# Scores between transposes and values: one run of projection products per step of differential attention, and another order of the opening

## The chip, the cores and the metric

The kernel runs on one core of one Trainium2 chip. The metric is the device time of one execution in microseconds; lower is better. The engines of the core are called as in the profile: PE (TensorE's matmuls) and PEld (its weight loads), DVE (VectorE), ACT (ScalarE), POOL (GpSimd) and SP (SyncE, which here only issues DMAs).

## The reference

Two decoder layers over 512 tokens of width 1024, each followed by a gated ConvFFN. The change touches only layer 0, the even layer: latent attention (MLA, 8 heads) and differential attention (4 heads) run behind one input projection, and their outputs go through one output projection.

```python
def even_mixer(h, w_in, cq_g, w_uq, ckv_g, w_ukv, ...):
    c_q, c_kv, k_rope, dq, dk, dv = split_cols(h @ w_in, EVEN_SPLITS)
    q = heads_first(rms_norm(c_q, cq_g) @ w_uq, MLA_HEADS)
    kv = heads_first(rms_norm(c_kv, ckv_g) @ w_ukv, MLA_HEADS)
    o_mla = mla_attention(q_nope, q_rope, k_nope, rope(k_rope, pos), v_mla)
    ...
    o_diff = diff_attention(dq[:, :, 0], dq[:, :, 1], dk[:, :, 0], dk[:, :, 1], dv, lam, slopes)
    o_diff = rms_norm(o_diff, subln_g) * (1.0 - lam_init)
    return jnp.concatenate([heads_last(o_mla), heads_last(o_diff)], axis=-1) @ w_out

def diff_attention(q1, q2, k1, k2, v, lam, slopes):   # per block of 128 queries
    p = probs(a1, k1) - lam * probs(a2, k2)           # two causal softmaxes with ALiBi
    return p @ v
```

## The kernel before

Weights and activations of the large products are split into two float32r parts, high and low, and a product is three matmuls: high by high, high by low, low by high (`mm3`, or `one_by_one`, which does the same one matmul at a time as a generator). Transposes, scores and values of the attentions are plain float32 matmuls. In the trace both kinds show as f32; the float32r ones are those with `xh`, `xl`, `wh`, `wl`, `omh`, `oml` and the like, below called projection products.

The even layer is written out by hand: inside `tc.manual_schedule` each engine runs its instructions in the order in which the code issues them. Layer 0 has four stretches before its ConvFFN:

1. **The opening.** Eight column blocks of the input are split and multiplied into four token tiles `ac` (`product_c`; tile 3 first). Each tile's mean squares (`squares_c`: ACT squares, then POOL adds and raises to the power -0.5), its norms (`norm_c` on DVE, into `ctok`), and its transposes with their copies and split (`turn_c`: PE, then ACT and DVE) follow. `square_x` makes the mean square of a row tile of x, for one tile on DVE at L1388. Between them stand matmuls of the first differential head's q and k (`diff_qk(0, z)`, output `aqk`), which a `Fill` object issues a few at a time, as `dq0(5)` does. Their weights are cast by ACT (`cast`, L1273) and their low part is made by DVE (`rest`, L1278). `rows` (L1526) spreads the row norms over the partitions with matmuls on `dv`, which DVE fills at L1512.
2. **Products of the latent heads** (`auq`, `auk`, `auv`).
3. **Latent attention**, 32 units, one per step, with projection products between as filling.
4. **Differential attention**, 16 units (`D_UNITS`: 4 heads, in each the query blocks 3, 2, 1, 0, so the width of the scores falls from 512 to 128). A unit m passes through `d_score` (PE, two matmuls into two banks `sps`), `d_softmax` (DVE table pass at L1210, ACT exponential at L1212), `d_combine` (DVE), `d_turn` (PE transposes into `tpp`), `d_copy`, `d_value` (PE, `o`), `d_out`, `d_norm`, and after the fourth unit of a head `d_finish` (PE transposes `tpo`, then a split by ACT and DVE). A step m works on several units at once, and `fill(n)` issues n projection products in each step: first the rest of the v and q/k projections of this attention, then half of the output projection (`ao`).

PSUM has eight banks with tags: three `a`, two `s`, one each of `t`, `o`, `n`. The scores use both banks `s`; `tpp` uses `t`; `tpo` uses `n` for heads 0 and 1 and `t` for heads 2 and 3. The last use of a bank must be read before its next matmul starts.

Of the kernel before, what the change touches and what calls it, by code (L numbers as in the profile page):

```python
# [19 lines left out]
P = 128  # L20
# [329 lines left out]
def trunk(tc, A, out):  # L350
# [3 lines left out]
    with ExitStack() as top:  # L354
# [105 lines left out]
        def split(h, l, src):  # L460
            ACT.copy(h, src)
            DVE.tensor_tensor(l, src, h.bitcast(F32), ALU.subtract)
# [729 lines left out]
        def even():  # L1192
            with ExitStack() as es:
# [32 lines left out]
                def diff_qk(h, z):  # L1226
                    acc = bank("a", "aqk")
                    wh, wl = W.next()
                    for k in range(KD):
                        yield from one_by_one(acc, wh[:, k * P:(k + 1) * P], wl[:, k * P:(k + 1) * P],  # L1230
                                              xh[:, k], xl[:, k], k == 0, k == KD - 1)
                    if z == 0:
                        DVE.scalar_tensor_tensor(dq[h], acc, -0.125, rbc, ALU.mult, ALU.mult)
                    else:
                        DVE.tensor_tensor(dk[h], acc, rbc, ALU.mult)
# [97 lines left out]
                def d_combine(m, between=None):  # L1333
# [9 lines left out]
                    DVE.scalar_tensor_tensor(s1[:, :w], s2[:, :w], v[:, 1], s1[:, :w], ALU.mult, ALU.add)  # L1343
                    d_s[m] = s1

                order = ExitStack()
                with ExitStack() as e1:
                    mp = e1.enter_context(tc.tile_pool(name="em", bufs=1, reuse_waits="tile"))
# [61 lines left out]
                    with ExitStack() as e2:  # L1410
# [7 lines left out]
                        def squares_c(i):  # L1418
                            a = acs[3 - i]
                            e = rx[:, 1, i:i + 1]  # L1420
                            ctoks[i] = mean_square(a[:, 0:256], e), mean_square(a[:, 256:384], e)

                        def norm_c(i):
                            a = acs[3 - i]
# [19 lines left out]
                        def turn_c(i):  # L1444
                            tp = bank("tn"[i % 2], "tc", 4, P)
                            for k in range(4):
                                PE.transpose(tp[:, k], ctoks[i][:, k], ident[:])
# [3 lines left out]
                            ACT.copy(mk[1][0:64, t], tp[0:64, 3])  # L1451

                        W.depth = 1
                        ones = dv[:, 1, :P]
# [38 lines left out]
                        norm_c(3)  # L1493
                        last_c(2)
                        squares_c(2)
                        square_x(0, False)
                        begun = cast(W)
                        rest(*begun)
                        W.load()
                        norm_c(2)  # L1500
                        last_c(1)
                        squares_c(1)
                        last_c(0)
                        norm_c(1)
                        squares_c(0)
                        dq0, dk0 = [Fill(diff_qk(0, z)) for z in range(2)]
                        dq0(8)
                        turn_c(3)
                        begun = cast(W)
                        norm_c(0)  # L1510
                        for i in ORDER:
                            DVE.tensor_scalar(dv[:, 3, i * P:(i + 1) * P], ident[:], rx[:, 0, i:i + 1], None,  # L1512
                                              ALU.mult)
# [122 lines left out]
                    for n in range(M + 2):  # L1636
# [17 lines left out]
                        if m == 1:  # L1654
                            d_combine(0)
# [5 lines left out]
                        if n + 1 >= M:  # L1661
                            d_score(m + 1)
# [28 lines left out]
                def d_turn(m):  # L1691
                    h, i = D_UNITS[m]
                    s = d_s.pop(m)
                    tp = bank("t", "tpp", 4, P)
                    for j in range(i + 1):
                        PE.transpose(tp[:, j], s[:, j * P:(j + 1) * P], ident[:])
                    return tp

                def d_copy(m, tp):
                    i = D_UNITS[m][1]  # L1700
# [25 lines left out]
                    DVE.scalar_tensor_tensor(o, o, d_r.pop(m)[:, 0:1], subg[0], ALU.mult, ALU.mult)  # L1726

                def d_finish(h):
                    tp = bank("n" if h < 2 else "t", "tpo", NT, P)
                    for i in range(NT):  # L1730
                        PE.transpose(tp[:, i], otoks[h][:, i], ident[:])
                    split(oD[0][:, h], oD[1][:, h], tp.rearrange("p a b -> p (a b)"))

                def normed(i, r, t):
# [26 lines left out]
                made = dict(zip((2, 3, 4, 5, 7, 8, 9, 11, 13, 15, 17), (W, W, W, W2, W2, W2, W, W, W, W, W)))  # L1761
                loads = list(made.values())
                quota = [16] + [12] * 8 + [9, 8, 8, 9, 12, 8, 5, 4, 9]
# [6 lines left out]
                for m in range(2, N + 4):  # L1770
                    if m - 2 < N:
                        tp = d_turn(m - 2)
                    if 0 <= m - 3 < N:
                        o = d_value(m - 3)
                    if m < N:
                        d_softmax(m)
                    if m - 2 < N:
                        d_copy(m - 2, tp)
                    if 0 <= m - 3 < N:
                        d_out(m - 3, o)  # L1780
                    if m - 1 < N:
                        d_combine(m - 1)
                    if begun:
                        rest(*begun)
                        begun = None
                    n = quota[m - 2]
                    fill((n + 1) // 2)
                    if m + 1 < N:
                        d_score(m + 1)
                    fill(n // 2)  # L1790
                    if 0 <= m - 4 < N:
                        d_norm(m - 4)
                        if m == N + 3:
                            fill.end()
                        if (m - 4) % 4 == 3:
                            d_finish((m - 4) // 4)
# [503 lines left out]
```

## Time and profile before

| | |
|---|---|
| median of 3 runs | 1128.19 us (1127.31 to 1129.4) |
| the profiled execution's own time | 1128.83 us |
| its span, first to last instruction | 1127.1 us |
| mean granted TensorE clock | 0.999 |
| PE busy | 1111.5 us, 99% of the span |
| DVE, ACT, POOL busy | 80%, 56%, 20% |
| chain that ended last | PE 93% |

A row of the timeline has the start in us from the span's start, the duration in us, the engine, the line, the operation, output and inputs with their shapes, the number of like instructions in the row, and in brackets the idle time of the engine before it and what ended it. One float32 matmul of the code is two instructions in the trace. Matmuls overlap in a pipeline, so their cost is read from one start to the next, not from their durations; the same holds in part for DVE, whose instructions start a little before the one ahead has ended.

### The profile page before, as it was taken

The numbers are of one execution on the slowest core, as the hardware profiler recorded it, in microseconds if no ns is written. First come the engines' busy times: TensorE is split into PE (matmuls) and PEld (weight loads), VectorE is DVE, ScalarE is ACT, GpSimd is POOL, SyncE is SP. The second block draws the span as 40 slices with busy tenths as digits, with TensorE's granted clock in tenths as the row PEclk, the third lists the DMA queues.
The fourth block names the chain that finished last, engine by engine and source line by source line (L and its number), as shares of the span: only waits on it lengthen the run. The fifth ranks groups of instructions, "written<-read, shape, count | busy, mean of one in ns | idle before, by whom it ended". The sixth has DMA issues, their size and how long they took to land.

```text
span 1127.1 us, 17789 instructions
## 1 busy us (share of the span) xinstructions
PE 1111.5 (99%) x6568; PEld 959.1 (85%) x6568; DVE 905.6 (80%) x1612; ACT 635.1 (56%) x1115; POOL 229.3 (20%) x295
## 2 busy tenths in 40 slices
PE   8999999999999999999999999999999999999997
PEld 8766676898999999888888877898989999988886
DVE  5676677589989999999873565577899999999996
ACT  5465555347566766466453464545456676655662
POOL 2533332233222211000020030002421221220002
PEclk9999999999999999999999999999999999999999
DMA  8699932263444236555735296222535332265551
GB/s 299 241 233 165 170 105 94 75 246 141 142 158 166 96 103 214 198 168 170 240 102 175 77 237 145 86 75 87 206 113 169 121 133 85 76 243 181 162 208 74
DMA packets 58503, 174.18 MB, mean 155 GB/s; under 512 B 6960, under 2 KB 9648, under 8 KB 58416
## 3 DMA queue, kind: packets, MB, share of 16 engines
q1 hardware_dynamic: 48736, 148.77, 38.3%
q0 software_dynamic: 7520, 20.98, 9.6%
q10 hardware_dynamic: 2160, 3.30, 1.0%
q8 instruction: 51, 0.84, 0.3%
q14 instruction: 36, 0.29, 0.1%
HBM read 156.75 MB, written 35.65 MB: 171 GB/s over the span
## 4 chain that ended last, share of the span: by engine, by line
PE 93%; DMA 2%; DVE 2%; POOL 1%; ACT 1%; issue 1%; SPq 0%; POOLq 0%; DVEq 0%; ACTq 0%
PE u L553 13%; PE u L554 13%; PE u L555 13%; PE acc L554 6%; PE acc L555 6%; PE acc L553 6%; PE apt L553 3%; PE apt L554 3%; PE apt L555 3%; PE sps L1403 1%; PE ao L553 1%; PE ao L554 1%; PE ao L555 1%; PE aqk L1220 1%; PE aqk L1224 1%; PE sps L1323 1%
## 5 line engine op out<-in xcount | busy, mean ns | idle before, releaser
L553 PE MATMUL u<-xh,wh 128*128 128x256 f32 (+1 forms) x664 | 212.3, 320 | 0.0
L554 PE MATMUL u<-xl,wh 128*128 128x256 f32 (+1 forms) x664 | 212.0, 319 | 0.0
L555 PE MATMUL u<-xh,wl 128*128 128x256 f32 (+1 forms) x664 | 211.6, 319 | 0.0
L315 DVE TENSOR_TENSOR wl<-wraw,wh 128x1024 fp32r<-128x1024 f32 x92 | 111.3, 1219 | 36.3 <-ACT wh L314 36.2
L731 DVE SCALAR_TENSOR_TENSOR y<-u,cw,y 128x511 f32<-128x511 f32 (+1 forms) x176 | 129.5, 746 | 11.3 <-ACT y L726 8.3
L314 ACT CAST wh<-wraw 128x1024 fp32r<-128x1024 f32 x92 | 95.4, 1050 | 75.9 <-PE apt L554 28.8
L555 PEld LDWEIGHTS u<-xh,wl 128*128 128x128 f32 x664 | 126.5, 190 | 8.9
L553 PEld LDWEIGHTS u<-xh,wh 128*128 128x128 f32 x664 | 126.6, 191 | 8.3
L554 PEld LDWEIGHTS u<-xl,wh 128*128 128x128 f32 x664 | 126.6, 191 | 8.1
L553 PE MATMUL u<-th,wh 128*128 128x256 f32 x416 | 117.8, 283 | 0.2 <-DVE u L926 0.2
L555 PE MATMUL u<-th,wl 128*128 128x256 f32 x416 | 117.7, 283 | 0.0
L554 PE MATMUL u<-tl,wh 128*128 128x256 f32 x416 | 117.7, 283 | 0.0
L863 ACT CAST wh<-wraw 128x1024 fp32r<-128x1024 f32 (+1 forms) x104 | 88.9, 875 | 36.4 <-DVE wraw L850 16.2
L715 DVE TENSOR_TENSOR wl<-wraw,wh 128x512 fp32r<-128x512 f32 (+1 forms) x117 | 107.5, 934 | 1.2 <-ACT wh L863 0.8
L715 POOL TENSOR_TENSOR wl<-wraw,wh 128x512 fp32r<-128x512 f32 x51 | 66.1, 1298 | 205.7 <-DVE wl L715 51.2
L554 PE MATMUL acc<-wl,gh 128*128 128x512 f32 (+1 forms) x250 | 97.1, 390 | 0.0
L555 PE MATMUL acc<-wh,gl 128*128 128x512 f32 (+1 forms) x250 | 96.6, 388 | 0.0
L553 PE MATMUL acc<-wh,gh 128*128 128x512 f32 (+1 forms) x250 | 94.9, 388 | 0.0
L726 ACT ACTIVATE y<-u,cw 128x512 f32<-128x512 f32 x88 | 67.9, 779 | 36.0 <-PE u L555 24.2
L553 PEld LDWEIGHTS u<-th,wh 128*128 128x128 f32 x416 | 79.8, 192 | 1.4 <-DVE u L926 0.6
L554 PEld LDWEIGHTS u<-tl,wh 128*128 128x128 f32 x416 | 79.8, 192 | 0.7
L555 PEld LDWEIGHTS u<-th,wl 128*128 128x128 f32 x416 | 79.8, 192 | 0.0
(370 smaller groups left out, 2574.3 us busy)
## 6 DMA issues: line engine op xcount, KB each, us to landing
wraw<-in_ffn_w_up SPq DMA_DIRECT2D x78, 512.0 KB, 4.3
wraw<-in_ffn_w_down SPq DMA_DIRECT2D x44, 512.0 KB, 3.5
summed<-in_ffn_w_up POOLq DMA_DIRECT2D x40, 256.0 KB, 7.8
wraw<-summed SPq DMA_DIRECT2D x20, 512.0 KB, 4.5
wraw<-in_od_w_dqk SPq DMA_DIRECT2D x12, 512.0 KB, 3.8
wraw<-in_ffn_w_down SPq DMA_DIRECT2D x22, 256.0 KB, 3.1
summed<-in_ffn_w_up POOLq DMA_DIRECT2D x10, 512.0 KB, 9.8
summed<-summed POOLq DMA_DIRECT2D x20, 256.0 KB, 8.9
```

The costliest lines, as they stand in the source:

```text
L314: self.nc.scalar.copy(h[:, :w], raw[:, :w])
L315: self.nc.vector.tensor_tensor(l[:, :w], raw[:, :w], h[:, :w].bitcast(F32), ALU.subtract)
L553: PE.matmul(o, lh, rh, start=first, stop=False, skip_group_check=more)
L554: PE.matmul(o, lh, rl, start=False, stop=False, skip_group_check=more)
L555: PE.matmul(o, ll, rh, start=False, stop=last, skip_group_check=more)
L715: return engine.tensor_tensor(o, a, b, ALU.subtract)
L726: ACT.activation(ys[n][:, z], us[n][z], AF.Identity, bias=cw[:, PAIRED[n], z, 3:4], scale=c[:, 2:3])
L731: DVE.scalar_tensor_tensor(y[:, z, d:], u[:, :S - d], c[:, 2 - d:3 - d], y[:, z, d:], ALU.mult, ALU.add)
L863: ACT.copy(ws[n][w][0][:, c], src)
L1220: PE.matmul(o, lh, rh, start=first, stop=False)
L1224: PE.matmul(o, ll, rh, start=False, stop=last)
L1323: PE.matmul(d_s[m][z][:, :w], dq[h][r, i * P:(i + 1) * P], dk[h][r, :w], start=True, stop=True)
```

## The change

In the opening, `squares_c` makes both sums of a tile with two adds and one power of two columns (before: an add and a power for each sum). The weights' `cast` and `rest` for `diff_qk(0, 0)` come before the DVE's `square_x(0)`. For head 0, `diff_qk` issues the eight products with the high weights of its first four blocks first, and the four with the low weights after them. `norm_c(1)` moves behind `turn_c(3)`; in `turn_c` the two ACT copies come before the split; the four DVE instructions that fill `dv` for `rows` move behind `turn_c(0)`. In differential attention the scores of unit m+1 stand between the transposes of unit m-1 and the values of unit m-2, and a step's projection products follow in one run; `d_finish` of head 2 uses a bank `s`, and its split moves behind the step's other work on DVE. The loop starts with unit 1 in place of unit 2, since the first steps now stand behind latent attention.

```diff
 def diff_qk(h, z):
-    for k in range(KD):
+    first = 4 if h == 0 else 0
+    for k in range(first):
+        c = slice(k * P, (k + 1) * P)
+        for n, x in enumerate((xh, xl)):
+            if k or n:
+                yield
+            PE.matmul(acc, wh[:, c], x[:, k], start=k == n == 0, stop=False)
+    for k in range(first):
+        yield
+        PE.matmul(acc, wl[:, k * P:(k + 1) * P], xh[:, k], start=False, stop=False)
+    for k in range(first, KD):
         yield from one_by_one(...)
 def squares_c(i):
-    ctoks[i] = mean_square(a[:, 0:256], e), mean_square(a[:, 256:384], e)
+    for n, c in enumerate((slice(0, 256), slice(256, 384))):
+        ...
+        ACT.activation(junk[:, :w], a[:, c], AF.Square, scale=w ** -0.5, accum_out=ms[:, n:n + 1])
+        POOL.tensor_tensor(v[:, n:n + 1], ms[:, n:n + 1], e, ALU.add)
+    POOL.tensor_tensor(r[:, :2], v[:, :2], mhalf[:, :2], ALU.pow)
+    ctoks[i] = r[:, 0:1], r[:, 1:2]
 def turn_c(i):
-    split(cT[0][:, :, t], cT[1][:, :, t], tp[:, 0:3])
     ACT.copy(mk[0][64:128, t], tp[64:128, 3])
     ACT.copy(mk[1][0:64, t], tp[0:64, 3])
+    split(cT[0][:, :, t], cT[1][:, :, t], tp[:, 0:3])
 # the opening's order
 squares_c(2)
-square_x(0, False)
 begun = cast(W)
 rest(*begun)
 W.load()
+square_x(0, False)
 norm_c(2)
 ...
 last_c(0)
-norm_c(1)
 squares_c(0)
 dq0(8)
 turn_c(3)
+norm_c(1)
 begun = cast(W)
+dq0(5)
+turn_c(2)
 norm_c(0)
+dq0(5)
+turn_c(1)
+rest(*begun)
+W.load()
+dq0(5)
+turn_c(0)
 for i in ORDER:
     DVE.tensor_scalar(dv[:, 3, i * P:(i + 1) * P], ident[:], rx[:, 0, i:i + 1], None, ALU.mult)
-dq0(5)
-turn_c(2)
-dq0(5)
-rest(*begun)
-W.load()
-turn_c(1)
-dq0(5)
-turn_c(0)
 # behind the last unit of latent attention
+tp = m_turn(M - 1)
+d_score(1)
+d_combine(0)
+d_softmax(1)
+m_copy(M - 1, tp)
+fill(12)
+tp = d_turn(0)
+d_score(2)
 o = m_values(3)
 # d_finish
-    tp = bank("n" if h < 2 else "t", "tpo", NT, P)
+    tp = bank("nnst"[h], "tpo", NT, P)
 # the loop of differential attention, now
+quota = [12, 12, 12, 12, 12, 12, 12, 12, 12, 12, 10, 9, 9, 9, 9, 6, 6, 6]
+for m in range(1, N + 3):
+    if 1 < m <= N:            tp = d_turn(m - 1)
+    if 1 < m < N - 1:         d_score(m + 1)
+    if 0 <= m - 2 < N:        o = d_value(m - 2)
+    if 4 < m < N + 2 and m % 4 == 3: fin = d_finish(m // 4 - 1)
+    if m <= N:                d_copy(m - 1, tp)
+    if m < N:                 d_combine(m)
+    if m + 1 < N:             d_softmax(m + 1)
+    if 0 <= m - 2 < N:        d_out(m - 2, o)
+    if 0 <= m - 3 < N:        d_norm(m - 3)
+    if 4 < m < N + 2 and m % 4 == 3: d_split(m // 4 - 1, fin)
+    if begun: ...             # rest
+    fill(quota[m - 1])
+    if m in made: ...         # cast, load
+fill.end()
+d_split(3, d_finish(3))
```

PE in differential attention, one step of head 1. Before, `tpp` are the transposes of one unit, `o` the values of the unit ahead of it, `sps` the scores of a later unit, `aqk` the projection products; a line of dots stands for five more products `aqk` of the same form:

```order
L1696 MATMUL tpp<-ident,s 128x128 x2
L1712 MATMUL o<-dv,pt 128x128 x3
L1220 MATMUL aqk<-xh,wh 128x512
...
L1323 MATMUL sps<-dqk_108 128x384 x2
L1220 MATMUL aqk<-xh,wh 128x512
...
L1696 MATMUL tpp<-ident,s 128x128
L1712 MATMUL o<-dv,pt 128x128 x2
```

The same place after the change (`tpo` are a finished head's transposes; the dots stand for eleven products `aqk`):

```order
L1361 MATMUL tpp<-ident,s 128x128 x2
L1333 MATMUL sps<-dqk_108 128x512 x2
L1736 MATMUL o<-dv,pt 128x128 x3
L1755 MATMUL tpo<-ident,otok_1474 128x128 x4
L1224 MATMUL aqk<-xh,wl 128x512
...
L1361 MATMUL tpp<-ident,s 128x128
L1333 MATMUL sps<-dqk_108 128x384 x2
```

A step had two runs of six products with the scores between; it now has one run of twelve, and the scores stand with the other float32 matmuls.

DVE in the opening, before: the second norm (`ctok` of tile 3), then `square_x(0)` (the row with `dv,lead`), then the low weights `wl` of the first q/k product, then the norms of tiles 2 and 1:

```order
L1440 SCALAR_TENSOR_TENSOR ctok<-ac,rr,cgain 128x128
L1388 ISA dv,lead<-X_77 128x1024
L1388 ISA lead 128x1
L1278 TENSOR_TENSOR wl<-wraw,wh 128x1024
L1433 SCALAR_TENSOR_TENSOR ra<-ac,lead,rtab 128x32
```

And after:

```order
L1467 SCALAR_TENSOR_TENSOR ctok<-ac,rr,cgain 128x128
L1288 TENSOR_TENSOR wl<-wraw,wh 128x1024
L1406 ISA dv,lead<-X_77 128x1024
L1406 ISA lead 128x1
L1460 SCALAR_TENSOR_TENSOR ra<-ac,lead,rtab 128x32
```

The low weights stand one DVE pass of 128x1024 earlier, and the norms of tile 2 where they stood.

More of the change, by code (lines that the diff above doesn't have):

```diff
@@ L1344, in d_combine, with d_turn @@
                     d_s[m] = s1
+                def d_turn(m):
+                    h, i = D_UNITS[m]
+                    s = d_s.pop(m)
+                    tp = bank("t", "tpp", 4, P)
+                    for j in range(i + 1):
+                        PE.transpose(tp[:, j], s[:, j * P:(j + 1) * P], ident[:])
+                    return tp
                 order = ExitStack()
@@ L1420, in squares_c @@
                             e = rx[:, 1, i:i + 1]
-                            ctoks[i] = mean_square(a[:, 0:256], e), mean_square(a[:, 256:384], e)
+                            ms, v, r = [chp.tile([P, w], F32, tag=tag, name=tag, bufs=n)
+                                        for tag, w, n in (("ms", 2, 6), ("rv", 4, 4), ("rr", 4, 4))]
+                            for n, c in enumerate((slice(0, 256), slice(256, 384))):
+                                w = c.stop - c.start
+                                junk = chp.tile([P, D], BF16, tag="junk", name="junk", bufs=1)
+                                ACT.activation(junk[:, :w], a[:, c], AF.Square, scale=w ** -0.5,
+                                               accum_out=ms[:, n:n + 1])
+                                POOL.tensor_tensor(v[:, n:n + 1], ms[:, n:n + 1], e, ALU.add)
+                            POOL.tensor_tensor(r[:, :2], v[:, :2], mhalf[:, :2], ALU.pow)
+                            ctoks[i] = r[:, 0:1], r[:, 1:2]
                         def norm_c(i):
@@ L1635, in even @@
                     o = None
-                    for n in range(M + 2):
+                    for n in range(M + 1):
                         if n + 6 in made:
@@ L1653, in even @@
                             next(lam)
-                        if m == 1:
-                            d_combine(0)
                         if n + 1 < M:
@@ L1660, in even @@
                         fill((4, 4, 3, 3, 3, 3, 2, 2)[n % 8] if n < M - 8 else 4 if n < M else 12)
-                        if n + 1 >= M:
-                            d_score(m + 1)
+                        if n + 1 == M:
+                            d_score(0)
                         if n % 8 == 3 and n > 8:
@@ L1689, in even @@
                 W2.pair = pair
[L1691 to L1697, printed above, removed]
                 def d_copy(m, tp):
@@ L1728, in d_finish, with d_split @@
                 def d_finish(h):
-                    tp = bank("n" if h < 2 else "t", "tpo", NT, P)
+                    tp = bank("nnst"[h], "tpo", NT, P)
                     for i in range(NT):
                         PE.transpose(tp[:, i], otoks[h][:, i], ident[:])
+                    return tp
+                def d_split(h, tp):
                     split(oD[0][:, h], oD[1][:, h], tp.rearrange("p a b -> p (a b)"))
@@ L1760, in even @@
                 fill.parts += [project(*e, 0) for e in early]
[L1761 removed]
+                made = dict(zip((1, 2, 3, 4, 6, 7, 8, 10, 12, 14, 16), (W, W, W, W2, W2, W2, W, W, W, W, W)))
                 loads = list(made.values())
[L1763 removed]
+                quota = [12, 12, 12, 12, 12, 12, 12, 12, 12, 12, 10, 9, 9, 9, 9, 6, 6, 6]
                 norms, turns = [], []
@@ L1769, in even @@
                 split(oM[0][:, 3], oM[1][:, 3], o)
-                for m in range(2, N + 4):
-                    if m - 2 < N:
-                        tp = d_turn(m - 2)
-                    if 0 <= m - 3 < N:
[L1774 to L1782, printed above, removed]
+                for m in range(1, N + 3):
+                    if 1 < m <= N:
+                        tp = d_turn(m - 1)
+                    if 1 < m < N - 1:
+                        d_score(m + 1)
+                    if 0 <= m - 2 < N:
+                        o = d_value(m - 2)
+                    if 4 < m < N + 2 and m % 4 == 3:
+                        fin = d_finish(m // 4 - 1)
+                    if m <= N:
+                        d_copy(m - 1, tp)
+                    if m < N:
+                        d_combine(m)
+                    if m + 1 < N:
+                        d_softmax(m + 1)
+                    if 0 <= m - 2 < N:
+                        d_out(m - 2, o)
+                    if 0 <= m - 3 < N:
+                        d_norm(m - 3)
+                    if 4 < m < N + 2 and m % 4 == 3:
+                        d_split(m // 4 - 1, fin)
                     if begun:
@@ L1785, in even @@
                         begun = None
[L1786 to L1796, printed above, removed]
+                    fill(quota[m - 1])
                     if m in made:
```

## The prediction

> **What bounds the kernel now.** I read the page first, then the windows over layer 0's attentions, then what PE waits for in them, and last the timelines. The page:
>
> ```profile
> span 1127.1 us, 17789 instructions
> PE 1111.5 (99%) x6568; PEld 959.1 (85%) x6568; DVE 905.6 (80%) x1612; ACT 635.1 (56%) x1115; POOL 229.3 (20%) x295
> ```
>
> PE is the bound, and only 15.6 us of the span are idle on it. A change of order can win back idle time, and time in which PE counts as busy but starts its matmuls further apart. The windows (stretch, its length, then busy time of PE, PEld, DVE, ACT, POOL, the clock, DMA) tell where the idle time lies:
>
> ```profile
> 25.00:42.50 17.50, 14.72 (x74) 11.35 (x73) 13.52 (x34) 9.65 (x26) 11.10 (x21) 1.00 0.39 130
> 135.00:153.00 18.00, 18.00 (x95) 12.93 (x94) 14.85 (x46) 9.76 (x29) 6.28 (x12) 1.00 0.72 135
> 153.00:172.00 19.00, 19.00 (x99) 13.79 (x98) 14.88 (x49) 10.25 (x30) 5.00 (x9) 1.00 0.25 84
> 172.00:188.00 16.00, 15.81 (x85) 10.96 (x84) 12.77 (x47) 9.41 (x29) 3.89 (x8) 1.00 0.30 101
> 188.00:203.00 15.00, 13.51 (x75) 11.03 (x74) 9.55 (x28) 5.23 (x16) 6.15 (x10) 1.00 0.25 77
> ```
>
> The opening (25 to 42.5) has 2.8 us of it, the end of differential attention (188 to 203) 1.5 us. In the middle of differential attention PE counts as full, so what is to be won there must come out of the spacing of starts. The clock is 1.00 throughout.
>
> **The opening.** PE's waits, and the rows of its path:
>
> ```profile
> PE aqk L1224 <- DVE wl L1278: 1.5, 1, 1.5
> PE tc L1447 <- ACT mk L1451: 1.2, 2, 0.9
> 24.05 1.05 ACT L1273 CAST wh<-wraw 128x1024 fp32r<-128x1024 f32 x1 [0.38 <-DMA wraw<-in_ev_w_dqk]
> 25.09 1.22 DVE L1388 CUSTOM_DVE_ANT_0 dv<-X 128x1024 f32<-128x1024 f32 x1
> 25.32 0.47 PE L1220 MATMUL aqk<-xh,wh 128*128 128x512 f32 x1
> 26.23 1.22 DVE L1278 TENSOR_TENSOR wl<-wraw,wh 128x1024 fp32r<-128x1024 f32 x1
> 26.31 1.19 POOL L468 TENSOR_TENSOR rv<-ms,lead 128x1 f32<-128x1 f32 x1
> 27.37 0.53 DVE L1433 SCALAR_TENSOR_TENSOR ra<-ac,lead,rtab 128x32 f32<-128x32 f32 x3
> 27.58 0.55 POOL L471 TENSOR_TENSOR rr<-rv,mhalf 128x1 f32<-128x1 f32 x1
> 28.09 0.19 POOL L468 TENSOR_TENSOR rv<-ms,lead 128x1 f32<-128x1 f32 x1
> 31.56 0.55 DVE L462 TENSOR_TENSOR oml<-tc,omh 128x384 fp32r<-128x384 f32 x1
> 32.02 0.52 DVE L1433 SCALAR_TENSOR_TENSOR ra<-ac,lead,rtab 128x32 f32<-128x32 f32 x3
> 33.44 0.86 DVE L1512 TENSOR_SCALAR dv<-ident,lead 128x128 f32<-128x128 f32 x4
> 37.74 1.05 PE L1526 MATMUL rows<-dv 128*128 128x128 f32 x8
> ```
>
> PE needs the low weights for its third product and has them only after `square_x(0)` (25.09) and `rest` (26.23). Now `rest` starts when the cast ends at 25.1, and eight products with the high weights stand ahead: from 25.32 they last until 27.2 (one start to the next is 0.23, the first 0.31), `rest` ends at 26.3. This wait goes. Next late is DVE, whose work up to `rows` I lay end to end with spacings from the rows: `rest` 1.14 (26.23 to 27.37), `square_x` 1.14 (25.09 to 26.23), a norm 1.42 (32.02 to 33.44), a split 0.46 (31.56 to 32.02).
>
> From 25.1: `rest` to 26.3, `square_x` to 27.4, norm of tile 2 to 28.95 (0.1 of it for POOL's power, below), split of tile 3 to 29.4, norm 1 to 30.9, split of tile 2 to 31.5 (its ACT copies and cast end at 31.0), norm 0 to 32.9. PE's transposes can then start at 27.2, 29.0, 30.9 and 33.0; its own work would allow 27.2, 28.8, 30.7 and 32.6. Behind the last come its transposes (four float32 matmuls at about 0.1) and eight products (1.94), so `rows` could start at 35.3. `dv` for it now waits for the split of tile 1 (0.46), a `rest` (1.14), the split of tile 0 and the first of four fills: 35.3 to 35.5. Before it was 37.74, so the term is **2.2 us**. The later casts, `rest`s and norms of rows shift with it: by the same spacings the second weights of `auq` are ready about 0.9 us ahead of their use.
>
> Bounds: at least 0.9 (each of the four norms late by another 0.3, the wait that POOL's power already cost one of them here), at most 2.8, all of PE's idle time in this window.
>
> POOL is the risk: its add at 26.31 took 1.19 us beside a DVE pass of 1.22, the like add at 28.09 took 0.19. Tile 2's two adds now fall beside `rest` and `square_x`, each ending with the DVE pass it meets: 26.35, 27.5, then the power (0.55) until 28.2, which is when DVE wants it. The Trainium skill, "SBUF — State Buffer" (section "SBUF: two separate sides"), says that a DVE instruction with two SBUF inputs holds the port pair it shares with GpSimd for its whole length and the other fully blocks. The trace agrees by the 1.19; if the power too had to wait out a pass, the term would be about 1.6.
>
> **Differential attention: the joined runs.** The rows of one step:
>
> ```profile
> 155.82 0.40 PE L1224 MATMUL aqk<-xh,wl 128*128 128x512 f32 x1
> 156.14 1.13 PE L1323 MATMUL sps<-dqk 64*128 64x512 f32 x4
> 157.20 0.50 PE L1220 MATMUL aqk<-xh,wh 128*128 128x512 f32 x1
> 157.54 0.39 PE L1222 MATMUL aqk<-xl,wh 128*128 128x512 f32 x1
> 157.77 0.39 PE L1224 MATMUL aqk<-xh,wl 128*128 128x512 f32 x1
> 158.47 0.39 PE L1224 MATMUL aqk<-xh,wl 128*128 128x512 f32 x1
> 158.70 0.60 PE L1731 MATMUL tpo<-ident,otok 128*128 128x128 f32 x4
> 64.97 0.27 PE L1603 MATMUL tpp<-ident,s 128*128 128x128 f32 x1
> 65.08 0.81 PE L1403 MATMUL sps<-mk,mq 128*128 128x384 f32 x2
> ```
>
> Within a run the starts are 0.23 apart. Ahead of the scores it is 0.32 (155.82 to 156.14), behind them 0.34 (157.20 to 157.54); ahead of transposes 0.23 (158.47 to 158.70). So scores in the middle of a run cost 0.09 + 0.11 = 0.20 us beyond themselves. Behind a transpose the scores follow after 0.11 (64.97 to 65.08, in latent attention), which is the transpose's own length: nothing extra. Thirteen steps have their scores moved: 13 x 0.20 = 2.6. Two more scores, those of the steps before, lose the 0.09 ahead of them: 0.2. Together **2.8 us**.
>
> The Trainium skill, "TensorE: Matmul & The Clock Gate" (section "Step-by-step: what each phase is for"), has the drain of one matmul overlap the fill of the next, so that the gap is the stream's length. By that a switch costs nothing and this term is 0; the 0.32 and 0.34 speak against it.
>
> **Differential attention: the waits.**
>
> ```profile
> 123.24 0.92 PE L1323 MATMUL sps<-dqk 64*128 64x384 f32 x4
> 124.09 0.66 PE L1603 MATMUL tpp<-ident,s 128*128 128x128 f32 x4
> 161.50 1.32 PE L1323 MATMUL sps<-dqk 64*128 64x384 f32 x4
> 162.75 0.50 PE L1220 MATMUL aqk<-xh,wh 128*128 128x512 f32 x1
> 179.74 1.52 PE L1323 MATMUL sps<-dqk 64*128 64x384 f32 x4 [0.19 <-DVE st L1210]
> 194.78 0.44 PE L1696 MATMUL tpp<-ident,s 128*128 128x128 f32 x2 [1.40 <-DVE odl L462]
> 140.82 0.69 DVE L1210 CUSTOM_DVE_ANT_0 s<-sps,alibi 128x512 f32<-128x512 f32 x1 [1.04 <-PE tpp L1696]
> 118.83 1.13 PE L1323 MATMUL sps<-dqk 64*128 64x512 f32 x4
> 199.28 0.38 PE L1712 MATMUL o<-dv,pt 128*128 128x128 f32 x2
> 202.75 0.63 PE L1731 MATMUL tpo<-ident,otok 128*128 128x128 f32 x4
> ```
>
> Scores of 384 need 0.85 us to the next start where nothing holds them (123.24 to 124.09); those at 161.50 took 1.25, those at 179.74 took 0.6 more by their durations (1.52 against 0.92), with 0.19 of idle time ahead. They wait for DVE to read the two banks `s`. In the new order a table pass is read out in the step ahead of the next scores, so that twelve products (2.85 us) lie between: 1.2 us go. The transposes at 194.78 wait 1.4 us for the bank `t` that the head's transposes hold until DVE's split; head 2 now takes a bank `s`, which the scores no longer want: 1.4 us go. Sum **2.6 us**.
>
> What is late next: at the end, PE reaches the last `tpo` twelve products behind the last values (0.14 + 2.85 = 3.0 us), while the chain `d_out`, square, POOL's add and power, `d_norm` took 3.5 us before (values at 199.28, `tpo` at 202.75, with thirteen products or 3.2 us of PE's work between). It costs 0.5 where it cost 0.3: −0.2. In the loop's first step DVE comes from the split of `oM`, and the scores may wait 0.1. So −0.3, at most −1.0.
>
> DVE must keep up. From 135 to 188 it is busy 42.5 of 53 us (14.85 + 14.88 + 12.77), in twelve steps. PE will need 53 − 12 x 0.20 − 1.2 = 49.4, so DVE may wait 0.57 us per step before it sets the pace. Its table pass needs scores that end 0.75 to 1.3 us into the step; ahead of it stand the copy and `d_combine`, 0.7 to 1.3 us. I expect 0.1 to 0.5 of waiting, and the splits, which it waited for long, now stand behind its other work.
>
> **The sum.** 2.2 + 2.8 + 2.6 − 0.3 = 7.3 us. Behind layer 0's attentions PE has hardly a wait and the same code, so I let the shift pass whole. 1128.83 − 7.3 = 1121.5; the profiled execution lies 0.64 above the median of 1128.19, and I take off about half of it: **1121.2 us**.
>
> **The rivals.**
> - *The switches only move.* The scores behind transposes pay ahead of the values what they paid in the run. Against it: the 0.109 of latent attention, whose scores are of another shape (128 rows). Then 2.8 is 0: 1124.0. Chance 0.10.
> - *DVE sets the pace, mildly.* Scores at a step's head make DVE wait there, as at 140.82 (1.04 us). With 1.2 us in each of twelve steps: 12 x (1.2 − 0.57) = 7.6 given back, 1128.8. Chance 0.08.
> - *The same, slower than before.* From 1.4 us per step on, when ACT's exponentials come late as well; with 1.6: 12 x 1.03 = 12.4, so 1133.6. For it: DVE runs in order, and `d_combine` of one unit stands ahead of the next table pass. Against: the slack above. Chance 0.07.
> - *DMA takes it back.* Layer 0's ConvFFN starts earlier than its weights land. Against: DMA's share of 0.25 there. Half the gain, 1124.9; chance 0.04.
>
> My forecast has 0.71. Its own bounds: 2.8 + 2.8 + 2.6 = 8.2 gives 1120.3, and with a scatter like that of the runs before (0.9 below their median to 1.2 above) 1119.2; above, 0.9 + 2.6 + 1.4 − 1.0 = 3.9 gives 1124.6. The first and the last rival lie near that, so the range is 1119.2 to 1125.0 and leaves out the two with DVE. Faster by over 0.2% (2.3 us, about what a measurement of this kernel tells from no change): 0.71 + 0.10 + 0.04 = 0.85; within 0.2%: 0.08; slower: 0.07.
>
> **What would show it.** In the profile after, `rows` should start near 35.4, no wait on the low weights be left, and the third and fourth transposes wait under 0.5. A run of twelve should take 2.85, scores of 512 1.06 behind transposes. From the first scores of head 0 (118.83 before) to the last `tpo` (202.75) there are 83.9 us; I expect 78.7. I am wrong if that stretch is over 81, if `sps` wait for L1210 in most steps, or if the time before the ConvFFN shrinks and the span does not.

## The result, and the profile after

| | us, median (lowest to highest, runs) | ratio to before (95%) |
|---|---|---|
| before | 1128.59 (1127.31 to 1134.99, 20) | |
| changed | 1126.74 (1124.32 to 1129.12, 20) | 0.9980 (0.9972 to 0.9989) |
| forecast | 1121.2 (range 1119.2 to 1125.0) | |

Faster, but by 1.9 us instead of 7.3. The profiled execution took 1129.12 us, the slowest of its 20 and as long as the one of before, so its rows show more than the median lost. The head of its page:

```profile
span 1127.1 us, 17795 instructions
PE 1113.0 (99%) x6568; PEld 961.1 (85%) x6568; DVE 905.7 (80%) x1612; ACT 634.5 (56%) x1115; POOL 220.9 (20%) x291
PE 80%; issue 9%; POOL 4%; DMA 3%; DVE 2%; ACT 1%; POOLq 0%; DVEq 0%; ACTq 0%; SPq 0%
```

The chain that ended last was 93% PE before; now it is 80%, and POOL has 4% of it. The opening, from PE's waits and the timeline:

```profile
PE aqk L1235 <- ACT wh L1283: 0.4, 1, 0.4
34.18 1.11 POOL L1585 COPY mk<-mk 64x512 f32<-64x512 f32 x1 [3.14 <-ACT mk L1476]
35.20 1.58 DVE L1547 TENSOR_SCALAR dv<-ident,lead 128x128 f32<-128x128 f32 x4
35.35 0.61 POOL L1586 COPY mk<-mk 64x512 f32<-64x512 f32 x1
35.63 1.70 PE L1553 MATMUL rows<-dv 128*128 128x128 f32 x8
117.19 1.13 PE L1333 MATMUL sps<-dqk 64*128 64x512 f32 x4
202.64 0.63 PE L1755 MATMUL tpo<-ident,otok 128*128 128x128 f32 x4 [0.34 <-DVE otok L1750]
```

`rows` start at 35.63 (37.74 before), and the waits for low weights and for the transposes are gone. But `rows` take 1.70 us (1.05 before), because the four fills of `dv` take 1.58 (0.86) beside POOL's copies. Head 0's first scores are 1.64 us earlier (118.83 before). The last `tpo` is only 0.1 us earlier: the stretch between them is 85.4 us, before 83.9, forecast 78.7, and the prediction had named a stretch over 81 as a sign that it is wrong. One step of it:

```profile
164.52 0.27 PE L1361 MATMUL tpp<-ident,s 128*128 128x128 f32 x1
164.72 0.92 PE L1333 MATMUL sps<-dqk 64*128 64x384 f32 x4
165.57 0.71 PE L1736 MATMUL o<-dv,pt 128*128 128x128 f32 x4
166.04 0.48 PE L1224 MATMUL aqk<-xh,wl 128*128 128x512 f32 x1
```

The scores start 0.20 behind a transpose that needs 0.11, and the four `o` take 0.47 where they needed 0.37. The 0.20 us that the scores cost inside a run of projections have only moved.

The largest hole lies at 146 us. POOL's last DMA issue of `summed`, its first power, DVE's first norm, PE's next transposes, and then the windows around it (stretch, length, PE busy and so on, the clock behind POOL's time):

```profile
143.71 0.81 POOL L425 DMA_DIRECT2D summed<-summed  x1 [4.89 <-PE o L1736]
144.88 0.57 POOL L471 TENSOR_TENSOR rr<-rv,mhalf 128x1 f32<-128x1 f32 x1
145.49 0.35 DVE L1750 SCALAR_TENSOR_TENSOR otok<-otok,rr,small 128x128 f32<-128x128 f32 x1 [5.76 <-POOL rr L471]
148.43 0.63 PE L1361 MATMUL tpp<-ident,s 128*128 128x128 f32 x4 [2.35 <-DVE s L1353]
146.08:149.50 3.42, 1.07 (x8) 0.93 (x8) 3.38 (x12) 0.71 (x3) 0.17 (x1) 1.00 0.74 161
149.50:152.91 3.41, 3.41 (x10) 2.37 (x9) 3.38 (x10) 2.36 (x8) 1.02 (x2) 0.50 0.38 105
```

POOL issues the stored sums of the ConvFFN's weights from the same queue as its arithmetic, so the first power comes when the last of these issues is through. DVE's first norm, now one step earlier, waits 5.76 us for it; `d_combine` stands behind it, and PE runs dry for 2.35 us. Then the clock is at 0.50 for 3.41 us.

### The profile page after: what moved, and what is told of

It is laid out like the page before. It is cut to its first block, busy times and chain, and to the rows that moved or that the text cites. A ratio compares the mean times of both kernels' runs of the same rounds, so it can differ in the third digit from the quotient of the medians.

```text
span 1127.1 us, 17795 instructions
## 1 busy us (share of the span) xinstructions
PE 1113.0 (99%) x6568; PEld 961.1 (85%) x6568; DVE 905.7 (80%) x1612; ACT 634.5 (56%) x1115; POOL 220.9 (20%) x291
## 4 chain that ended last, share of the span: by engine, by line
PE 80%; issue 9%; POOL 4%; DMA 3%; DVE 2%; ACT 1%; POOLq 0%; DVEq 0%; ACTq 0%; SPq 0%
PE u L553 13%; PE u L554 13%; PE u L555 13%; PE acc L554 6%; PE acc L555 6%; PE acc L553 6%; PE apt L553 3%; PE apt L554 3%; PE apt L555 3%; POOL summed L425 2%; PE ao L553 1%; PE ao L555 1%; PE ao L554 1%; PE cp L1990 1%; DMA summed<-in_ffn_w_up 1%
```

## The experiments

Times below are medians against runs of the kernel before on the same chip; the ratio in brackets is not that of the medians, since slow runs move it more. The stretch is that from head 0's first scores to the start of the last `tpo` (the expectations of e9_no_power and e11_best_order count to the last of its four matmuls, 0.36 us later).

### Theory A: POOL's queue; and the two halves apart

Theory A was that the missing gain is the wait for POOL. Rival B: DVE cannot keep the new order's pace. Rival: the parts are worth less than forecast. `e1_norms_late` postpones the first head's norms:

```diff
-                    if 0 <= m - 3 < N:
-                        d_norm(m - 3)
+                    for u in {3: (), 4: (), 5: (0, 1), 6: (2, 3)}.get(m, (m - 3,)):
+                        if 0 <= u < N:
+                            d_norm(u)
```

> The changed kernel with the first head's norms put one to two steps later (units 0 and 1 in step 5, 2 and 3 in step 6); all else as changed. Theory A (POOL's queue: the first power waits behind the DMA issues of the stored sums, the first norm waits for it, DVE runs in order and PE runs dry): DVE's wait of 5.76 us for `rr`, PE's 2.35 us ahead of the transposes and the clock's dip behind it are gone; the stretch from head 0's first scores to its last `tpo` goes from 85.4 to 80.5 to 81.5 us, the time from 1126.7 to 1122 to 1124.5 us. Rival B (DVE cannot keep the pace of the new order): PE waits for DVE somewhere else in the loop for about as long, the stretch stays above 84 us and the time within 1126 to 1128 us.

Measured: 1124.36 against 1127.98 (0.9969, 0.9957 to 0.9980), stretch 81.1 (118.08 to 199.20), no wait of PE in it but 0.4 us for the last `tpo`. B falls: DVE keeps pace.

`e2_open_only` is before with the change's opening, `e3_loop_only` before with its loop.

> The kernel before with the opening's part of the change alone. If the opening's 1.5 to 1.6 us (first scores of head 0 at 118.83 before, 117.19 changed) pass through whole, the time is 1.6 us below before (ratio 0.9986) and the stretch of differential attention stays at 83.9 us. If the loop before takes it back (its norms stand a step later, but POOL's queue ends at the same time whatever the opening does), the first norm waits for up to 1 us, the stretch grows by as much and the time is within 0.6 us of before.

> The kernel before with the loop's part of the change alone. By the prediction's sum the loop is worth 5.1 us (1123.5; stretch 78.7). Theory A with switches that only move (joined runs worth 0, removed waits 2.6, late norm 2 to 4): stretch 83 to 85 us, time -0.5 to +1.5 us from before, the first norm waits 4 to 6 us for POOL. If joined runs are worth their 2.8 us after all and only the late norm hides it: stretch 81 to 82 us, time 2 to 3 us below before.

The opening alone: 1127.25 (0.9994, 0.9985 to 1.0003), 0.7 us instead of 1.6, stretch unchanged. Its runs fall into two groups, seven at 1126.6 to 1127.3 and four at 1128.4 to 1128.5. The loop alone: 1125.81 (0.9987, 0.9978 to 0.9996), 2.2 us, stretch 81.1. This loop has its norms at the changed place, and its first one waited only 0.8 us, since the last of POOL's issues came at 140.0 and not at 143.7. So the wait is not in every execution. A stretch of 81 to 82 and a gain of 2 to 3 us were what this run's expectation had for joined runs that are worth their 2.8 us; the next part shows that they are not.

### Where the joined runs' 2.8 us went

The traces of before and e1_norms_late have the same 429 rows of PE's matmuls in the stretch. Counted from each start to the next, the projection products take 52.84 us before and 50.12 with the change: 2.7 less, as forecast. The transposes `tpp` and the values `o` take 15.15 and 18.10: 2.95 more. What the stretch gained is in the scores (13.07 and 11.84) and in `tpo` with the wait behind them (2.87 and 1.07), together 3.0 us: the removed waits.

`e4_scores_first` is e1_norms_late with `d_score(m + 1)` ahead of `d_turn(m - 1)`.

> As e1_norms_late, and in each step of the differential loop the next unit's scores stand ahead of the transposes instead of behind them: they follow a run of projections. If a switch between the scores (64 rows) and matmuls of 128 rows costs 0.1 us on each side wherever it stands: run to scores 0.32, scores to transposes 0.1 more than the transposes need elsewhere, the sum of a step unchanged, PE's stretch within 0.5 us of e1_norms_late but for waits; DVE waits for the scores (6.1 us in all as changed) fall below 2 us, which PE feels only if DVE was late. If scores behind transposes were the cheaper place: 0.1 us dearer in each of 13 steps, 1.3 us.

Its timeline for one step, from the start of a run of twelve:

```profile
158.11 0.48 PE L1224 MATMUL aqk<-xh,wl 128*128 128x512 f32 x1
161.06 0.92 PE L1333 MATMUL sps<-dqk 64*128 64x384 f32 x4
161.90 0.33 PE L1361 MATMUL tpp<-ident,s 128*128 128x128 f32 x1
162.07 0.61 PE L1736 MATMUL o<-dv,pt 128*128 128x128 f32 x4
162.44 0.48 PE L1224 MATMUL aqk<-xh,wl 128*128 128x512 f32 x1
```

The run takes 2.95 instead of 2.85 and the transpose 0.17 instead of 0.11; `o` is back at 0.37. The price is paid on both sides of the scores, wherever they stand. The stretch is 81.0 us, the time 1125.37 (0.9977, 0.9968 to 0.9985). DVE's waits for scores fell from 6.1 to 4.0 us, not below 2, and PE felt nothing of it.

`e10_rows_128`, which ran once, asks what the price is for. It takes e8_fills_early (below) and gives each score product all 128 rows of `dq` and `dk`, not the half `r`.

> As e8_fills_early, but each of the two score products of a unit takes all 128 rows of queries and keys instead of its 64 (so both give the sum of the two score maps: the output is another). The two products can no longer lie beside each other, so the scores themselves take about twice as long; what counts is the spacing at their edges. Theory E (the 0.2 us per group of scores is the price of going from 128 rows to 64 and back): transposes to scores 0.11 instead of 0.20, scores to values without the 0.10 that `o` now takes more, so four `o` 0.37 instead of 0.47 and eight 0.81 instead of 0.91. Rival (it comes with the bank or with the order of the groups): 0.20 and 0.47 as before.

```profile
160.37 0.27 PE L1361 MATMUL tpp<-ident,s 128*128 128x128 f32 x1
160.48 1.46 PE L1333 MATMUL sps<-dqk 128*128 128x384 f32 x4
161.77 0.61 PE L1736 MATMUL o<-dv,pt 128*128 128x128 f32 x4
162.13 0.47 PE L1224 MATMUL aqk<-xh,wl 128*128 128x512 f32 x1
```

Transposes to scores 0.11, `o` 0.36: both edges are free. The scores themselves take 1.29 instead of 0.85. So the 0.2 us is the price of going to pairs of products of 64 rows and back. The run takes away both the 64 rows and the pair that lies side by side; which of them costs is not separated. The Trainium skill, "TensorEngine Tiling (Array Packing)" (section "Tiling Modes"), says that a change of the tiling mode drains TensorE; the trace agrees in so far as the scores cost 0.09 on the way in and 0.10 on the way out.

### Theory C: the start of the program

Six of the nine profiles with ten warm-up products, those of e1_norms_late, e3_loop_only and e4_scores_first among them, had the full clock for good only from 10.2 to 10.9 us, the other three (before, changed, e2_open_only) by 6.2. In e9_no_power the `ac` products start 0.35 us apart until 10.2 and 0.19 apart after it. With a late clock the last `ac` product starts at 26.3 to 26.6 instead of 24.9. Theory C: the change's opening shows the start's 1.6 us, which before's opening hides. The edit, in four kernels:

```diff
-WARM = 10
+WARM = 12
```

`e5_warm_before` has it on before, `e6_warm_open` on e2_open_only, `e7_warm_norms` on e1_norms_late. `e8_fills_early` also moves the four fills of `dv` on DVE up, to right behind `norm_c(0)`.

> The kernel before with 12 warm-up products instead of 10 (PE then has work without a gap from 1.05 us until its first real product at about 6.2). In the six profiles so far the clock reached full speed at 5.0, 6.1 and 5.8 us in three and at 10.3 to 10.7 in three; in the latter the last `ac` product starts 1.6 us later (26.35 to 26.57 instead of 24.87). Theory C (the start's clock decides what the opening's change is worth): full speed from 7.5 us at the latest in every execution, last `ac` at 24.8 to 25.4. Before's opening does not care, since its PE then waits for the low weights and for the transposes: first `auq` at 42.4 to 42.6 as in both kinds, time within 0.4 us of before. Rival: the start has nothing to do with the warm-up; last `ac` at 24.87 or 26.5 as chance has it, time equal too.

> The opening's part of the change alone (as e2_open_only), with 12 warm-up products. Theory C: last `ac` at 24.8 to 25.4, first `auq` at 40.2 to 40.7; none of its runs in a second group 1.6 us above the others (e2_open_only: seven runs at 1126.6 to 1127.3, four at 1128.4 to 1128.5); time 1.0 to 1.6 us below e5_warm_before. Rival (the opening is worth about 0.7 us whatever the start): 0.5 to 0.9 us below e5_warm_before, scatter of 1.9 us as in e2_open_only.

> e1_norms_late (the changed kernel with the first head's norms later) with 12 warm-up products. Theory C: 0.5 to 0.9 us below e1_norms_late's distance from before, so 4.1 to 4.6 us below before (1123.4 to 1123.9 where before is at 1128.0), scatter below 1.5 us. Rival: as e1_norms_late, 3.6 us below before.

> As e7_warm_norms, with the four fills of `dv` for `rows` moved up on DVE, from behind the splits of tiles 1 and 0 to right behind the last norm. In all kernels with the changed opening two of the four fills took 0.63 to 0.64 us instead of 0.28, beside copies on POOL, and `rows` took 1.70 us instead of 1.05. Theory D (DVE's fills and POOL's copies hold each other up; POOL's copies start when tile 1's or 0's transposes are copied out, behind the new place of the fills): fills 0.28 each (0.86 for the four), `rows` without a wait, first `auq` 0.6 us earlier than e7_warm_norms, time 0.3 to 0.6 us below it. Rival: `rest` and the casts, now 0.8 us later, hold `auq`'s weights up; first `auq` no earlier, time equal.

| | us | its before | ratio (95%) |
|---|---|---|---|
| e5_warm_before | 1128.10 | 1128.28 | 0.9997 (0.9988 to 1.0006) |
| e6_warm_open | 1126.97 | 1128.28 | 0.9991 (0.9982 to 1.0000) |
| e7_warm_norms | 1123.63 | 1128.28 | 0.9964 (0.9951 to 0.9976) |
| e8_fills_early | 1122.80 | 1128.28 | 0.9956 (0.9943 to 0.9970) |

All ten profiles with twelve warm-ups, of these and later kernels, have the full clock by 7.05 us and the last `ac` at 24.8 to 25.1. Before gains nothing from it. But one expectation missed: its first `auq` came at 40.55, not at 42.4, because its first loads had landed earlier; its loop then gave 1.2 us back (stretch 85.1), as its own first norm waited 1.1 us for POOL and the scores 0.8 for DVE. So these times do not show that before's opening hides a late start. By these medians the opening is worth 1128.10 − 1126.97 = 1.1 us (0.7 in e2_open_only; the intervals of both reach from nothing to 1.7 or 2.0), and the slower group of e2_open_only is gone.

In e8_fills_early the fills take their 0.86 us and `rows` wait for nothing:

```profile
32.26 0.86 DVE L1541 TENSOR_SCALAR dv<-ident,lead 128x128 f32<-128x128 f32 x4
34.54 1.05 PE L1553 MATMUL rows<-dv 128*128 128x128 f32 x8
```

That is 0.9 us at the first `auq` (39.30 against 40.18) and 0.8 us in time, more than the 0.3 to 0.6 expected. Theory D holds.

### How much of it is the norms

`e9_no_power` leaves out POOL's add and power for head 0's units.

> The changed kernel, norms at their place, but the add and the power for head 0's four units are left out (a constant takes their place, so head 0's values are not normed by their square). Theory A (the first norm waits for POOL, whose queue holds the stored sums' DMA issues until 139 to 145 us): without POOL in the chain the norms wait for nothing, PE's wait of 2.35 us and the clock's dip are gone, the stretch is 81.3 to 81.7 us (scores' start to the last `tpo`'s start, 85.8 as changed, by this measure 81.5 with norms late), the time that of e1_norms_late against its before, 3 to 4 us below. Rival (the norms' place in DVE's order does it, whatever POOL): stretch above 83 us.

The stretch is 81.1 us and PE's wait gone, yet the time is 1125.91 (0.9980, 0.9971 to 0.9989), that of the changed kernel. This speaks against Theory A as the main cause. Three kernels that differ only in the norms then had the longer warm-up: `e12_warm_changed` (the change as it is), `e13_warm_no_power`, `e14_warm_norms_again` (e7_warm_norms once more).

> The changed kernel with 12 warm-up products, nothing else. Theory A (the wait for POOL's queue costs PE 1 to 2.5 us and, in some executions, a dip of the clock): median 1 to 3 us above e14_warm_norms_again, with scatter of 2 us or more, since the queue ends between 138 and 145 us; the fastest run equals e14's. Rival (the late norm is the profiled execution's mishap only, the missing gain is the start's): the scatter goes with the start, median within 0.7 us of e14.

> As e12_warm_changed, head 0's add and power on POOL left out as in e9_no_power (head 0's values are not normed by their square). Theory A: as e14_warm_norms_again within 0.5 us, 1123.3 to 1124.2 where before is at 1128. If its time stays 1.5 us or more above e14, something else than POOL's power makes norms at that place dear.

> The kernel of e7_warm_norms once more, on the same chip as the two others: 1123.5 to 1124.8, 4.0 to 4.7 us below before.

| | us | its before | ratio (95%) |
|---|---|---|---|
| e12_warm_changed | 1124.50 | 1128.37 | 0.9965 (0.9953 to 0.9978) |
| e13_warm_no_power | 1124.52 | 1128.37 | 0.9965 (0.9953 to 0.9978) |
| e14_warm_norms_again | 1124.18 | 1128.37 | 0.9967 (0.9954 to 0.9979) |

No difference, so with the longer warm-up Theory A falls as the cause of the median. In e12_warm_changed POOL's issues ended earlier, and the first norm's wait was short enough for PE to feel nothing (stretch 81.1):

```profile
138.64 0.81 POOL L425 DMA_DIRECT2D summed<-summed  x1 [3.85 <-DMA summed<-summed]
140.42 0.35 DVE L1750 SCALAR_TENSOR_TENSOR otok<-otok,rr,small 128x128 f32<-128x128 f32 x1 [1.48 <-POOL rr L471]
```

Last, the change as it is, with the longer warm-up, and with late norms and the old warm-up, on one chip:

> The changed kernel once more, beside the two that follow on the same chip. If the start decides: 1125.5 to 1127 in the median, scatter 2.5 us or more, 1 to 2 us above e16_warm_changed_again. If it was the chip: within 0.6 us of e16.

> e12_warm_changed once more: 1124 to 1125, 3.4 to 4.2 us below before, scatter at most 2.3 us.

> e1_norms_late once more (old warm-up, norms late). If the start decides and the norms matter in few executions: within 0.7 us of e15_changed_again in the median, but without the slowest runs (none above 1126.5). If POOL's queue still costs the changed kernel its part at the old warm-up: 1.5 us or more below e15.

| | us (lowest to highest) | its before | ratio (95%) |
|---|---|---|---|
| e15_changed_again | 1125.75 (1123.75 to 1131.44) | 1128.22 | 0.9984 (0.9973 to 0.9995) |
| e16_warm_changed_again | 1123.93 (1123.57 to 1130.31) | 1128.22 | 0.9970 (0.9959 to 0.9981) |
| e17_norms_late_again | 1125.25 (1123.67 to 1125.70) | 1128.22 | 0.9969 (0.9957 to 0.9981) |

The longer warm-up takes 1.8 us off the median, late norms 0.5; by the ratios it is 1.6 and 1.7. The intervals of these three overlap, so the times alone do not tell the two causes apart. The slowest runs, 1131.44 of e15_changed_again and 1130.31 of e16_warm_changed_again (a scatter of 6.7 us where at most 2.3 was expected), have no trace.

The profiles show the start by itself. With the changed opening, the changed order of the loop and a stretch of 81.1, the four with a late clock (e1_norms_late, e9_no_power, e15_changed_again, e17_norms_late_again) took 1125.28 to 1125.65 us, the five with the longer warm-up (e7_warm_norms, e12_warm_changed, e13_warm_no_power, e14_warm_norms_again, e16_warm_changed_again) 1123.53 to 1124.28: about 1.5 us. The starts of e15_changed_again, then of e16_warm_changed_again, each by its first two rows on PE and by windows:

```profile
1.06 3.92 PE L398 MATMUL warm<-zero 128*128 128x128 f32 x20 [1.06 <-DVE zero L395]
6.23 0.46 PE L553 MATMUL ac<-wh,xh 128*128 128x416 f32 x1 [1.25 <-ACT wh L1388]
4.06:7.48 3.42, 1.77 (x11) 1.31 (x11) 1.70 (x3) 3.41 (x6) 0.00 (x0) 1.00 1.04 374
7.48:10.89 3.41, 3.41 (x12) 3.23 (x11) 3.05 (x6) 2.61 (x6) 0.00 (x0) 0.50 1.05 389
6.20:26.50 20.30, 19.87 (x96) 19.29 (x97) 12.73 (x25) 13.33 (x31) 5.63 (x14) 0.92 0.96 343
```

```profile
1.05 5.05 PE L398 MATMUL warm<-zero 128*128 128x128 f32 x24 [1.05 <-DVE zero L395]
6.16 0.45 PE L553 MATMUL ac<-wh,xh 128*128 128x416 f32 x1
7.48:10.89 3.41, 3.41 (x19) 3.38 (x19) 3.06 (x7) 2.63 (x6) 0.00 (x0) 1.00 1.06 396
116.25 1.13 PE L1333 MATMUL sps<-dqk 64*128 64x512 f32 x4
197.37 0.63 PE L1755 MATMUL tpo<-ident,otok 128*128 128x128 f32 x4 [0.36 <-DVE otok L1750]
```

In the first, the clock is full from 4.07 us; PE then stands idle for 1.25 us ahead of its first real product, and the clock is halved for the 3.41 us from 7.48. The mean of 0.92 over 20.3 us makes 1.6 us. In the second, the warm-up lasts until the data is there. Its stretch is 81.1 us.

The other five late starts look different: their ten products end at 5.7, PE is idle for 0.35 to 0.52 us, and the clock is not full before 10.2 to 10.7. The changed kernel and e2_open_only have the same gaps (0.45 and 0.50) and the full clock by 6.2. What differs is where the steps of the clock fall, which lie 3.41 us apart: in the three early starts one falls at 5.0 to 6.1 us, in the six late ones, counted back from the full clock, at 3.4 to 4.1 and at 6.8 to 7.5. With twelve, e7_warm_norms and e12_warm_changed have gaps of 0.74 and 0.62 us, but the full clock by 4.6, and they keep it.

`e11_best_order` is e8_fills_early with the scores ahead of the transposes.

> e8_fills_early with the scores ahead of the transposes (the order of e4_scores_first). If the switch costs 0.03 to 0.06 us less a step there, as the profiles of e1_norms_late and e4_scores_first read: stretch 0.1 to 0.3 us shorter than 81.48, time 0.2 to 0.5 us below e8_fills_early. If the 1 us that e4_scores_first lost behind the attentions (first `acc` to first `apt` 132.2 us against 131.4) belongs to this order: 0.5 to 1 us above e8_fills_early.

1122.91 against 1127.86 (0.9955, 0.9942 to 0.9967), stretch 81.0: no better than e8_fills_early, and no worse; the 0.2 to 0.5 us that it should win did not show. Either of them beats both kernels.

## Why the prediction was wrong

**The joined runs** (2.8 us) are the step that failed, and its rival "The switches only move" (chance 0.10) was right. The row on which I relied, scores 0.11 behind a transpose in latent attention, is of scores with 128 rows. I noted the other shape and gave the objection a chance of 0.10; e10_rows_128 shows that the free edge belongs to that shape. A run of twelve does take 2.85, as forecast, and the products of the stretch 2.7 us less; the transposes and values beside the scores took 2.95 more. So the term is 0. That rival's 1124.0 is close to what the change gives with the longer warm-up, 1124.5 and 1123.9, in part by luck: its opening is 1.1 us too large and its waits are too small.

**The waits less what is late next** (2.6 − 0.3 = 2.3) were right: the stretch shrinks by 83.9 − 81.1 = 2.8 where POOL's queue does not disturb it, and the count of starts puts all of that down to the scores and `tpo`. DVE kept the pace, as the slack of 0.57 us a step said, and the last `tpo` waits 0.34 to 0.37. Both rivals with DVE fall, and nothing speaks for the one with DMA: from the first product of the ConvFFN to the last matmul it is 887.3 us before and 887.4 changed.

**The opening** (2.2) is mis-sized, at 1.1 by medians with a clean start. The mechanism is right in each row: `rows` at 35.63 where 35.3 to 35.5 was forecast, no wait for low weights, no waits at the transposes. What was missing: the fills were priced by their old 0.86, without the POOL copies that now run beside them; e8_fills_early wins 0.8 us by that alone. Besides, 2.2 was measured against one execution of before with first `auq` at 42.53; that of e5_warm_before had it at 40.55.

**Not in the sum at all** was the start. Where the clock comes late, the changed opening pays: first `auq` at 41.6 to 41.9 (e1_norms_late, e4_scores_first, e9_no_power, e15_changed_again, e17_norms_late_again), against 40.1 to 40.5 with twelve warm-ups. Before's opening had 42.53 with a clean start and 42.37 (e3_loop_only) with a late one, but 40.55 in e5_warm_before; that it hides a late start is the reading of one pair. The late start accounts for about 1.5 of the 2.2 us between 1124.5 and the 1126.74 of the result in an execution that has it, and it does not reach that median: 13 of the 20 runs of the result lie above 1126.5, where the late profiles took 1125.3 to 1125.7. In e15_changed_again, the same kernel again, it is 3 of 11, in e17_norms_late_again none of 5. POOL's queue is the only further cause that a trace shows, that of the profiled run; the other runs have no trace, so what put them there stays open.

**"DVE must keep up" left out POOL** ahead of DVE's first norm, moved a step forward. It cost the profiled execution 85.4 − 81.1 = 4.3 us: 2.35 of waiting and the clock's dip. It was the only one of the five profiles with the changed loop and norms in which PE felt it; without it the profiled execution would have been near 1124.8, by subtraction.

So the account is 1.1 + 2.8 = 3.9 us with the longer warm-up (measured 3.9 and 4.3), less about 1.5 where the start is late and up to 4.3 where POOL's queue holds the first norm. How often each came in the runs of the result is open. One slip in the prediction's sums decides nothing: 1120.3 − 0.9 is 1119.4, not 1119.2.

## What to carry to other kernels

A change that removes a wait can expose what the wait hid: before summing, look at several executions for what scatters ahead of it, here the clock at the start and the landing of loads. A matmul's price at its edges belongs to its shape; a row of another shape is no row for it. When an instruction is moved forward on an engine that works in order, look at the whole queue of the engine that feeds it, DMA issues included.

## What the runs showed of the hardware

- Going from float32 matmuls of 128 rows to a pair of products of 64 rows and back costs 0.09 and 0.10 us here; between matmuls of 128 rows the same places cost nothing (0.11 and 0.36 us in e10_rows_128).
- The clock was halved for 3.41 us behind windows of the same length in which PE was busy for 1.07 us (changed, one gap of 2.35) and for 1.77 us (e15_changed_again, gaps of 1.25 and 0.40). In the profile of before, a window with 2.21 us was followed by full speed:

```profile
4.99:8.40 3.41, 2.21 (x12) 1.75 (x11) 2.64 (x5) 3.40 (x8) 0.00 (x0) 1.00 1.02 377
```

The Trainium skill, "TensorE: Matmul & The Clock Gate" (section "HAM oscillation — how this bites in real kernels"), gives as the rule that no idle gap should exceed about 3.4 us. These gaps were shorter and the clock fell, so here that rule was not enough. For the fall, the busy share of a window fits every window of the 19 traces: 31% and 52% were too little, 65% was enough, and so was 54% (1.83 us from 1112.14 in e11_best_order). For the rise at the start no share separates them: windows with 2.96 us (changed, from 2.73) and 3.01 us (e15_changed_again, from 0.66) were enough, one with 3.03 us (e9_no_power, from 3.38) was not.
- DVE's fills of 128x128 took 0.64 instead of 0.28 us each where a copy on POOL ran beside them, two of four; POOL's copies of 64x512 took 0.61 to 1.63 us in the changed kernel.
